# The order of a first stage, its loads and its band means, and a half group of matmuls at a later joint

## The chip, the cores and the metric

The kernel runs on one core of one Trainium2 chip. The metric is the device time of one execution in microseconds (us). Three runs of the kernel before gave 1173.47, 1173.22 and 1169.82 us: the median is 1173.22 us.

## The reference

Two layers of a diffusion backbone, for 512 latent tokens and 256 context tokens of 1024 channels. Layer 0 mixes tokens by centred means over windows of 2, 4, 8 and 16 tokens (one window for each group of 256 channels), layer 1 by attention. Cut to layer 0's first half:

```
sh1, sc1, gt1, sh2, sc2, gt2 = split(silu(cond) @ w_ada + b_ada, 6)     # one cond for latents, one for context
h = rms_norm(x, g_mix_pre) * (1 + sc1) + sh1
y = concat_g((window_mean_g(h_g) - h_g) @ w_pool[g]) * pool_scale        # four groups of 256 channels
x = x + gt1 * rms_norm(y, g_mix_post)
m = square(relu((rms_norm(x, g_mlp_pre) * (1 + sc2) + sh2) @ w_mlp_in)) @ w_mlp_out
x = x + gt2 * rms_norm(m, g_mlp_post)
```

Layer 1 has attention (`w_qkv`, `w_o`) in the place of the pooling, the same MLP, and for the output only the latents. All data are float32.

## The kernel before

**Numbers in two halves.** A product is made of float32r operands: each operand is split into a high part (a CAST on ACT) and a low part (a subtraction on DVE), and three matmuls (high·high, high·low, low·high) stand for one. "hi" and "lo" below are these two steps; `hH`/`hL` (in `ra`) hold an activation's halves, `rb` and `units` hold weights'.

**Tokens and stages.** Tokens lie in tiles of 128: tiles 0 to 3 are latents, 4 and 5 context. The first stage, which the diff rewrites, does this: (1) load x; normalise each tile; (2) multiply each tile by a band matrix, which gives "window mean minus the token" for every channel block k of 128 (PSUM tiles `psm` for latents and `psc` for context, opened for two blocks at a time); (3) load the conditioning weights `w_ada` in 20 loads of 1 MB and form shift, scale and gate: `ada_mm` (tile `psada`), `ada_rows` (a transpose on DVE), `ada_sel` (four tiny matmuls), then `mods`, `avec`, `minus` on DVE; (4) `centred`: scale and shift the means into `hH` (ACT) and `hL` (DVE); (5) the mixer `pool_a` (tile `pspool`): for each token tile and each group g six matmuls of 256 columns with the pooling weights; (6) its mean square, gate (`psg` are the gate's rows), residual, and the next norm; (7) `turn0`/`mod0`: transposes (`psx`), second modulation and split; (8) the first MLP group `psin`, begun in pieces of two channel blocks as they come ready.

**The joint.** At about 820 us attention's output projection (`psy`) ends and layer 1's MLP begins: token tiles 2 and 3 are normalised, turned and modulated (`norm_pair`) while the first MLP group `Inner(0, ...)` works on tiles 0 and 1 (`part(0, f)`), then on tiles 2 and 3 (`part(1, f)`). The group after it is multiplied in 512 columns at once.

**What sets the order.** Steps are put in a list with times (`st.at`), sorted and emitted in that order. A scheduler then moves instructions unless they are kept in program order; `Kept` keeps all of PE's instructions up to time 48 of the list and DVE's and ACT's up to 47.3 (`ordered`, `mixed`). Loads go through SP, in program order while `pinned`; a load waits until its buffer is free. Conditioning loads use a pool of four 1 MB buffers (`rawe`); the three buffers of `rawp` hold the pooling weights, two copies of the means (`stage`) and the MLP weights.

Of the kernel before, what the change touches and what calls it, by code (L numbers as in the profile page):

```python
# [37 lines left out]


# [29 lines left out]
def backbone(ctx: ExitStack, tc, x, ctx_in, w_ada, w_pool, pool_scale, w_qkv, g_q, g_k, w_o, w_mlp_in,  # L69
# [48 lines left out]

    def raw_load(src, pool=None):
        t = (pool or pools[0]).tile([P, 2048], F32, tag="raw", name="raw")  # L120
        d = sy.dma_start(t, src)
        if pinned[0]:
            tc.keep_in_program_order(d)
        return t
# [94 lines left out]
    def ada_mm(i, m, j, w=2):  # L219
        ps = psB.tile([P, 512], F32, tag="b", name="psada")  # L220
        kn = 2048 // (w * P)
        for z in range(KT // kn):
            raw = raw_load(w_ada[i, m, j + z]).rearrange("p (k n) -> p k n", n=w * P)
            for k in range(kn):
                at = kn * z + k
                q = 32 * (at % 4)
                te.matmul(ps[q:q + 32, 0:w * P], cond[:, at, :], raw[:, k, :], start=(at < 4), stop=(at >= 4))  # L227
        rowsd[i, m, j] = ps, w
# [12 lines left out]
    def ada_sel(i, m, j):  # L241
        ps, rows, w = rowsd.pop((i, m, j))
        out_ = ps[:, 0:2 * w]
        ada_turn(out_, rows.rearrange("p (b a x) -> p a x b", a=4, x=32)[:, :, 0:2, :], 2)
        ada_out(i, m, j, out_, 2, w)
# [52 lines left out]
    def gate_rows(i, m, ci, halves=(0, 1)):  # L298
        gc = gate_cols(i, m, ci, *((4 * halves[0], 4 * halves[-1] + 4)))
        for h in halves:  # L300
            ps = psB.tile([P, 512], F32, tag="b", name="psg")
            for k in range(4):
                te.matmul(ps[:, k * P:(k + 1) * P], gc[:, 4 * h + k:4 * h + k + 1].broadcast_to([P, P]), ident,
                          start=True, stop=True)
            sc.copy(gate[:, ci, 512 * h:512 * h + 512], ps)
# [16 lines left out]

    slot = [0] * NL + [1] * (NT - NL)
# [11 lines left out]
    def modulated_pair(t, i, s, hi, lo, works, wide, fine, on_act):  # L335
# [16 lines left out]
        for q in range(4):  # L352
# [13 lines left out]
            elif q % 2:  # L366
                ks = slice(2 * q - 2, 2 * q + 2)
                h = works[q // 2].rearrange("p (k n) -> p k n", n=256)
                sc.copy(place(hi, ks), h)
                ve.tensor_tensor(out=place(lo, ks), in0=h, in1=place(hi, ks), op=ALU.subtract)  # L370
# [11 lines left out]
    def mod0(t, q, on_act=(True, False)):  # L382
        ci, ps = 0 if t < NL else 1, turned.pop((t, q))
        for kk in range(2):
# [3 lines left out]
            if on_act[kk]:  # L388
# [5 lines left out]
        hi, lo = (z.rearrange("p k (h q n) -> p k q h n", h=2, n=P)[:, ks, t // 2] for z in (hH, hL))  # L394
        sc.copy(hi, h)
        ve.tensor_tensor(out=lo, in0=h, in1=hi, op=ALU.subtract)
# [25 lines left out]
    stage = {}  # L422

    def band_ev(k, q, on_act):
        if k not in stage:
            z = rawp.tile([P, 2048], F32, tag="raw", name="stage")
            stage[k] = z[:, 0:2 * TOK].rearrange("p (u n) -> p u n", n=TOK)
        t0, ln = SEGS[q]
        (sc.copy if on_act else ve.tensor_copy)(stage[k][:, :, t0:t0 + ln], (lat, con)[q][k])
        if q:  # L430
            for u in range(2):
                means[k + u] = [stage[k][:, u, t0:t0 + ln] for t0, ln in SEGS]

    rs, mix, yg, first = {}, {}, {}, []
# [7 lines left out]
    def centred(k, part):  # L442
        for ci, (t0, ln) in enumerate(SEGS):
            hi, lo, m = hH[:, k, t0:t0 + ln], hL[:, k, t0:t0 + ln], means[k][ci][:, 0:ln]
# [34 lines left out]
    def pool_a(t, gs=range(4), small_banks=False):  # L479
        if t not in mix:  # L480
            if small_banks:
                mix[t] = [psB.tile([P, 512], F32, tag="b", name="pspool") for _ in range(2)]
            else:
                pp_ = psA.tile([P, 2, 512], F32, tag="a", name="pspool")
                mix[t] = [pp_[:, 0, :], pp_[:, 1, :]]
        sl = slice(t * P, (t + 1) * P)
        for g in gs:
            seq = [(a, b, k) for k in (2 * g, 2 * g + 1) for a, b in ((hH, wp3H), (hH, wp3L), (hL, wp3H))]
            for n, (a, b, k) in enumerate(seq):
                te.matmul(mix[t][g // 2][:, (g % 2) * 256:(g % 2 + 1) * 256], a[:, k, sl], b[:, k, :],  # L490
                          start=(n == 0), stop=(n == len(seq) - 1))

    def pool_ms(t):
        pss = mix[t]
        ss = sm_tile("ss")
        for q in range(2):
            mean_square(pss[q], ss[:, q:q + 1])
        rs[t] = rstd(ss, 2)

    def pool_c(t):  # L500
        for q in range(2):
            sc.copy(accv[:, t, 512 * q:512 * q + 512], mix[t][q])
            mix[t][q] = accv[:, t, 512 * q:512 * q + 512]

    def pool_b(t, qs=range(2)):
        for q in qs:
            gated(t, accv[:, t, :], mix[t][q], 512 * q, 512 * q + 512)
# [22 lines left out]
    def norm_pair(t, i, s, hi, lo, wide, fine, on_act):  # L530
        modulated_pair(t, i, s, hi, lo, [accv[:, t, :], accv[:, t + 1, :]], wide, fine, on_act)
# [6 lines left out]
    def chunks1(g):  # L538
        if g == 0:
            return [[(0, 0, 0, 256)], [(1, 0, 256, 256)]], [(0, 2, 256, 0)]  # L540
# [4 lines left out]
    class Inner:  # L545
        def __init__(self, g, w, aH, aL, hid, chunks_of, ntok):
            self.w, self.a, self.ntok = w, (aH, aL), ntok
# [4 lines left out]
        def part(self, c, f, ks=range(KT)):  # L552
            (wH, wL), (aH, aL) = self.w, self.a
            if f not in self.ps:
                self.ps[f] = psA.tile([P, 2, 512], F32, tag="a", name="psin")
            ps, fs = self.ps[f], slice(f * P, (f + 1) * P)
            for k in ks:
                for n, (w, a) in enumerate(((wH, aH), (wH, aL), (wL, aH))):
                    for bank, o, t0, ln in self.chunks[c]:
                        start = k == 0 and n == 0  # L560
                        if ln is None:
                            ln, rhs = 256, a[:, k].rearrange("p (h q n) -> p q h n", h=2, n=P)[:, t0]
                            start = start and (f, bank) not in self.opened
                            self.opened.add((f, bank))
                        else:
                            rhs = a[:, k, t0:t0 + ln]
                        te.matmul(ps[:, bank, o:o + ln], w[:, k, fs], rhs, start=start,  # L567
                                  stop=(k == KT - 1 and n == 2), skip_group_check=len(ks) < KT)
# [157 lines left out]

    st = Steps()
    for t in range(NT):
        st.at(4.6 + 1.3 * t, rows_a, t)
    landing = ((19.3, 21.4, 22.4), (23.8, 25.9, 27), (27.1, 28.15, 28.7), (28.9, 30.0, 30.5), (31.4, 32.4, 33.4),  # L730
               (33.7, 34.8, 35.2), (40.6, 42.65, 43.9), (44.2, 46.25, 47.2),
               (47.75, 48.5, 49.5), (52.8, 53.2, 54.7), (60.5, 61.5, 62), (62.9, 63.9, 64.4), (65.2, 66.2, 66.7), (67.7, 68.7, 69.2))
    for zs, (m, j, w) in zip(landing, CONDITIONING):
        for z, fn, also in zip(zs, (ada_mm, ada_rows, ada_sel), ((w,), (), ())):
            st.at(z, fn, 0, m, j, *also)
    st.at(0, ordered.__setitem__, 0, True)
    st.at(0, mixed.__setitem__, 0, True)
    st.at(47.3, mixed.__setitem__, 0, False)
    st.at(48, ordered.__setitem__, 0, False)
    for t, z in enumerate((7.8, 9.7, 11.2, 12.7, 14.2, 16)):  # L740
        st.at(z, rows_b, t)
    for k in (0, 2):
        st.at(7.9, band_open, k)
    for t, z in enumerate((8.6, 9.9, 11.3, 13, 14.6, 18.2)):
        st.at(z, band_mm, t, range(4))
    for q, k, z in ((0, 0, 14.9), (0, 2, 14.9), (1, 0, 19.35), (1, 2, 19.35)):
        st.at(z, band_ev, k, q, k == 0)
    for k in (4, 6):
# [741 lines left out]
```

## Time and profile before

| | value |
|---|---|
| median of three runs | 1173.22 us |
| the profiled execution, own time | 1175.43 us |
| its span, first to last instruction | 1173.6 us |
| PE busy | 1147.6 us, 98% of the span |
| DVE busy | 934.4 us, 80% |
| ACT busy | 625.9 us, 53% |
| mean granted TensorE clock | 0.993 |

The profile is of one execution. Engines: PE is TensorE (PEld its weight loads), DVE VectorE, ACT ScalarE, POOL GpSimd, SP the queue that issues transfers. Times within it count from the span's start. In a line of the order of time the columns are start, duration, engine, source line, operation, output tile `<-` input tiles, shape, count, and in brackets the idle time ahead of it and what ended that. In the first stage most instructions carry the line of the helper `Kept` (L65 before), so tiles tell them apart. A float32 matmul with a full-precision operand (`psada`, `psc`, `psg`) shows as two records. In the table of stretches PEclk is the granted clock as a share of full speed.

### The profile page before, as it was taken

What the parts mean: (1) busy time and instruction counts of PE and PEld (TensorE: products, weight loads), DVE (VectorE), ACT (ScalarE), POOL (GpSimd) and SP (SyncE); (2) the same over time, 40 slices, a digit from 0 to 9 for tenths busy, and PEclk for the clock granted to TensorE, in tenths of its full rate; (3) what the DMA queues carried; (4) which work ended last, traced back from release to release, by engine and by line L of the source; (5) the groups of instructions that cost most, each with busy time, mean ns of one, the idle gap of its engine ahead of it and who ended that gap; (6) DMA issues with size and microseconds to landing.
All of it is one profiled execution on the core that took longest, in us unless ns stands there. A gap on an engine that the chain in (4) does not pass through costs nothing.

```text
span 1173.6 us, 15880 instructions
## 1 busy us (share of the span) xinstructions
PE 1147.6 (98%) x6124; PEld 993.3 (85%) x6124; DVE 934.4 (80%) x1518; ACT 625.9 (53%) x1067; POOL 68.6 (6%) x120
## 2 busy tenths in 40 slices
PE   7899999999999999999999999999899999999997
PEld 5679898899898988998888889998888888888886
DVE  4587687989988998897777599877687779778876
ACT  4576655454454435555585367753676436535522
POOL 2030000000000000000242200001100000000001
PEclk9899999999999999999999999999999999999999
DMA  9885114343444434343423100115134124304212
GB/s 368 329 321 181 50 59 144 117 155 129 144 144 144 144 116 147 115 144 126 180 72 108 37 1 37 37 73 214 73 135 153 59 85 144 108 36 144 108 36 108
DMA packets 25517, 147.32 MB, mean 126 GB/s; under 512 B 2785, under 2 KB 5217, under 8 KB 9698
## 3 DMA queue, kind: packets, MB, share of 16 engines
q1 hardware_dynamic: 25442, 146.32, 34.5%
q8 instruction: 48, 0.79, 0.3%
q14 instruction: 27, 0.22, 0.1%
HBM read 138.96 MB, written 7.34 MB: 125 GB/s over the span
## 4 chain that ended last, share of the span: by engine, by line
PE 49%; issue 42%; POOL 3%; DVE 3%; DMA 2%; ACT 1%; SPq 0%; POOLq 0%; DVEq 0%; ACTq 0%
PE pso L822 22%; PE psin L691 18%; PE psin L567 3%; PE psq L1067 2%; DMA raw<-in_w_ada 1%; PE pspool L65 1%; POOL rs L185 1%; PE psada L65 1%; PE pspool L490 1%; POOL rs L1076 1%; DMA xr<-in_x 1%; PE psada L227 1%; DVE ra L65 0%; POOL ms L183 0%; ACT junk L170 0%
## 5 line engine op out<-in xcount | busy, mean ns | idle before, releaser
L822 PE MATMUL pso<-units,rb 128*128 128x512 f32 x1152 | 278.2, 392 | 0.0
L822 PEld LDWEIGHTS pso<-units,rb 128*128 128x128 f32 x1152 | 214.8, 188 | 41.2
L273 DVE SCALAR_TENSOR_TENSOR rows<-raw,cond,rows 128x256 f32<-128x256 f32 x280 | 126.8, 476 | 2.0
L834 DVE TENSOR_TENSOR acc<-acc,pso 128x512 f32<-128x512 f32 x129 | 85.2, 675 | 41.2 <-PE pso L822 41.0
L567 PE MATMUL psin<-ra,rb 128*128 128x512 f32 (+1 forms) x432 | 104.7, 343 | 1.8 <-ACT ra L364 1.6
L926 PE MATMUL pso<-units,pairs 128*128 128x512 f32 x336 | 82.3, 389 | 0.0
L567 PEld LDWEIGHTS psin<-ra,rb 128*128 128x128 f32 x432 | 71.2, 193 | 11.3 <-ACT ra L364 1.9
L567 PE MATMUL psin<-ra 128*128 128x512 f32 x256 | 80.4, 389 | 0.0
L926 PEld LDWEIGHTS pso<-units,pairs 128*128 128x128 f32 x336 | 63.1, 188 | 13.1
L930 DVE TENSOR_TENSOR acc<-acc,pso 128x512 f32<-128x512 f32 x72 | 48.7, 681 | 28.8 <-PE pso L926 28.8
L183 POOL TENSOR_SCALAR ms<-ss 128x1 f32<-128x1 f32 x20 | 10.7, 533 | 998.0 <-ACT junk L170 943.9
L691 PE MATMUL psin<-ra,units 128*128 128x384 f32 x336 | 65.6, 337 | 0.4 <-ACT psin L703 0.4
L691 PE MATMUL psin<-sums,units 128*128 128x384 f32 x336 | 63.9, 337 | 0.0
L691 PEld LDWEIGHTS psin<-ra,units 128*128 128x128 f32 x336 | 59.7, 188 | 3.9 <-ACT psin L703 0.9
L691 PEld LDWEIGHTS psin<-sums,units 128*128 128x128 f32 x336 | 58.9, 188 | 1.7
L143 DVE TENSOR_TENSOR units<-raw,units 128x1024 fp32r<-128x1024 f32 (+2 forms) x49 | 55.1, 1149 | 3.9 <-ACT units L140 3.7
L567 PEld LDWEIGHTS psin<-ra 128*128 128x128 f32 x256 | 48.1, 188 | 9.9
L140 ACT CAST units<-raw 128x1024 fp32r<-128x1024 f32 (+2 forms) x49 | 46.8, 995 | 14.3 <-PE pso L822 10.2
L567 PE MATMUL psin<-rb 128*128 128x512 f32 (+1 forms) x144 | 53.4, 372 | 0.2 <-DVE rb L365 0.2
L832 ACT COPY acc<-pso 128x512 f32<-128x512 f32 x48 | 27.1, 587 | 49.0 <-PE pso L822 48.6
L1067 PE MATMUL psq<-units,ra 128*128 128x512 f32 x216 | 51.6, 392 | 0.0
L567 PE MATMUL psin<-rb,ra 128*128 128x512 f32 x128 | 49.8, 389 | 0.0
(280 smaller groups left out, 2344.6 us busy)
## 6 DMA issues: line engine op xcount, KB each, us to landing
raw<-in_w_ada SPq DMA_DIRECT2D x48, 1024.0 KB, 5.1
raw<-in_w_mlp_in SPq DMA_DIRECT2D x32, 1024.0 KB, 4.9
raw<-in_w_mlp_out SPq DMA_DIRECT2D x32, 1024.0 KB, 5.8
raw<-in_w_qkv SPq DMA_DIRECT2D x6, 1024.0 KB, 4.8
spill<-xr SPq DMA_DIRECT2D x10, 512.0 KB, 4.9
xr<-spill SPq DMA_DIRECT2D x10, 512.0 KB, 6.6
raw<-in_w_o SPq DMA_DIRECT2D x4, 1024.0 KB, 4.9
xr<-in_x SPq DMA_DIRECT2D x4, 512.0 KB, 6.2
```

The source lines that it names most:

```text
L65: return lambda *args, **kw: self.tc.keep_in_program_order(f(*args, **kw))
L140: a = sc.copy(hi, raw)
L143: b = ve.tensor_tensor(out=lo, in0=raw, in1=hi, op=ALU.subtract)
L273: ve.scalar_tensor_tensor(out=r, in0=raw[:, k, :], scalar=cond[:, k, c:c + 1], in1=r, op0=ALU.mult, op1=ALU.add)
L567: te.matmul(ps[:, bank, o:o + ln], w[:, k, fs], rhs, start=start, stop=(k == KT - 1 and n == 2), skip_group_check=len(ks) < KT)
L691: te.matmul(bank, w[k], a[k], start=start and k == 0 and m == 0, stop=stop and k == 3 and m == 2, skip_group_check=True)
L822: te.matmul(pss[h][:, 0:cols[h][1]], a[:, f, ts_], w[:, f, cols[h][0]:sum(cols[h])], start=(n == 0 and not seeded[t]), stop=(n == len(seq) ...
L832: sc.copy(d, ps)
L834: ve.tensor_tensor(out=d, in0=d, in1=ps[:, 0:w], op=ALU.add)
L926: te.matmul(ps, a, w, start=(m == 0), stop=(m == len(seq) - 1))
L930: ve.tensor_tensor(out=M[n][:, t], in0=M[n][:, t], in1=ps, op=ALU.add)
L1067: te.matmul(ps, a[:, k, sl], w[:, k % 4, :], start=(k == 0 and n == 0), stop=(k == KT - 1 and n == 2))
```

## The change

**First stage.** The conditioning loads take seven buffers: a list `turns` says for each of the 20 loads whether it goes to `rawe` (0) or to `rawp` (1), and the 1 MB of the first MLP weights is loaded behind the twelfth conditioning load, where it stood behind the eighteenth. The means no longer use `rawp`: `band_ev` copies those of all eight blocks (before: of blocks 0 to 3) from PSUM into `acc`, whose normalised rows have been read by then. The mixer works on tiles 5, 4 and 0 together as groups of `hH`/`hL` become ready, then on 1, 3 and 2. From list time 24.5 on, everything up to the end of the first MLP group is emitted in the order of one table, `FIRST`, and kept in it on PE, DVE and ACT (`ordered` and `mixed` end at 100). A halved load (`mm:SH1_0a`) and each of gate, split, evacuation and modulation is a word of its own in it.

**Joint.** The second MLP group of layer 1 has half of its weights split earlier (`half_early`), and its product for tiles 0 and 1 (24 matmuls of 256 columns) is put into the joint; a `paired` group keeps both halves f in one PSUM tile, in 256-column pieces. The split of the upper half of tiles 0 and 1 (`upper_half`) is emitted later, and the first group's product is cut in two for it. In `squares` both activations of the first two groups come after all of a group's matmuls.

```diff
+FIRST = """
+psc45 ev6 mm:SH1_0a ev4c psc67 mm:SH1_0b ev6c rows:SH1_0 mm:SC1_2 sel:SH1_0 rows:SC1_2 mods:SH1_0 sel:SC1_2 hi:0
...
     def raw_load(src, pool=None):
+        if pool is None and turns:
+            pool = (pools[0], rawp)[turns.pop(0)]
...
     def band_ev(k, q, on_act):
-        if k not in stage:
-            z = rawp.tile([P, 2048], F32, tag="raw", name="stage")
...
+        to = accv[:, (0, NL)[q]:(NL, NT)[q], P * k:P * k + 256]
+        (sc.copy if on_act else ve.tensor_copy)(to, (lat, con)[q][k].rearrange("p u (a n) -> p (u a) n", n=256))
...
-    def pool_a(t, gs=range(4), small_banks=False):
+    def pool_a(t, g):
         if t not in mix:
-            if small_banks:
+            if t in (4, 1):
                 mix[t] = [psB.tile([P, 512], F32, tag="b", name="pspool") for _ in range(2)]
...
     def chunks1(g):
-        if g == 0:
-            return [[(0, 0, 0, 256)], [(1, 0, 256, 256)]], [(0, 2, 256, 0)]
+        if g < 2:
+            return [[(0, 0, 0, 256)], [(0, 256, 256, 256)]], [(0, 1, 512, 0)]
...
+            if self.paired and not self.ps:
+                t = psA.tile([P, 2, 512], F32, tag="a", name="psin")
+                self.ps = {q: t[:, q:q + 1, :] for q in range(2)}
...
+    turns.extend((0, 0, 0, 0, 1, 1, 0, 0, 1, 0, 0, 1, 0, 0, 1, 0, 0, 1, 0, 0))
...
-    for z, t, g in ((30.6, 4, 0), (32.5, 4, 1), (35.4, 4, 2), (36.2, 5, 0), (36.3, 5, 1), (36.4, 5, 2), (42.6, 4, 3), (42.62, 5, 3)):
-        st.at(z, pool_a, t, (g,), t == 4)
...
+    for n, what in enumerate(FIRST.split()):
+        st.at(24.5 + n / 1000, step, what)
+    st.at(100, ordered.__setitem__, 0, False)
+    st.at(100, mixed.__setitem__, 0, False)
...
         def squares(inner, q):
+            for f in range(2) if inner.paired else ():
+                for c in range(2):
+                    if (c, f) not in begun[inner]:
+                        inner.part(c, f)
             for f in range(2):
-                inner.part(len(inner.chunks) - 1, f)
+                if not inner.paired:
+                    inner.part(0, f)
                 sc.activation(F[:, q, f, :], inner.relu(f), AF.Square)
...
-        wi = [None, w_in(1, 1, ins[1], True)]
+        put((hi[:, :, P:], lo[:, :, P:]), raw1[0][:, :, P:], True)
...
+    def half_early():
+        hi, lo = (rb[:, z:z + 1024].rearrange("p (k n) -> p k n", n=P) for z in (4096, 5120))
+        sc.copy(hi, raw1[0][:, :, 0:P])
...
+        at(41.65, upper_half)
         for f in range(2):
-            at((41, 42)[f], lambda *a: first1[0].part(*a), 0, f)
+            for h in range(2):
+                at(41.7 + f / 10 + h, lambda *a: first1[0].part(*a), 0, f, range(4 * h, 4 * h + 4))
...
+        for h in range(2):
+            at((47.5, 47.6)[h], lambda ks: first1[1].part(0, 0, ks), range(4 * h, 4 * h + 4))
```

PE before, from the first mixer matmuls of the first stage on (`psada<-raw,cond` is a load's product, `psada<-rows,sel` and `psada<-work,sel` are `ada_sel`, `pspool` is the mixer):

```order
L65 MATMUL pspool<-rb,ra 128x256 x6
L65 MATMUL psada<-raw,cond 32x256 x8
L65 MATMUL pspool<-rb,ra 128x256 x6
L65 MATMUL psada<-rows,sel 32x2x2 x4
L65 MATMUL psada<-raw,cond 32x256 x8
L65 MATMUL psada<-rows,sel 32x2x2 x4
L65 MATMUL pspool<-rb,ra 128x256 x24
L65 MATMUL psada<-raw,cond 32x512 x8
L65 MATMUL pspool<-rb,ra 128x256 x12
```

PE in the same place with the change:

```order
L87 MATMUL psada<-raw,cond 32x256 x16
L87 MATMUL psada<-rows,sel 32x2x2 x4
L87 MATMUL pspool<-rb,ra 128x256 x12
L87 MATMUL psada<-rows,sel 32x2x2 x4
L87 MATMUL psada<-raw,cond 32x256 x8
L87 MATMUL pspool<-rb,ra 128x256 x6
L87 MATMUL psada<-rows,sel 32x2x2 x4
L87 MATMUL psada<-raw,cond 32x512 x4
L87 MATMUL pspool<-rb,ra 128x256 x18
L87 MATMUL psada<-raw,cond 32x512 x4
L87 MATMUL pspool<-rb,ra 128x256 x12
```

The first mixer matmuls moved behind two more load products, and 36 mixer matmuls (tiles 5, 4 and 0) now stand ahead of the first gate load's second half, where 12 stood ahead of the whole load.

PE at the joint before, around the transposes of tiles 2 and 3 (`psin_7408` and `psin_7442` are the two halves f of the first group, `psx` the transposes):

```order
L567 MATMUL psin_7442<-rb_100 128x256
L567 MATMUL psin_7442<-ra_99,rb_100 128x256
L350 MATMUL psx_7475<-ident_87,acc_86 128x128 x3
L350 MATMUL psx_7480<-ident_87,acc_86 128x128 x3
L350 MATMUL psx_7485<-ident_87,acc_86 128x128 x3
L350 MATMUL psx_7490<-ident_87,acc_86 128x128 x3
L567 MATMUL psin_7408<-ra_99,rb_100 128x256
```

With the change (`psin_7420` is the first group, `psin_7513` the second):

```order
L608 MATMUL psin_7420<-ra_99,rb_100 128x256
L608 MATMUL psin_7513<-rb_100 128x256
L608 MATMUL psin_7513<-ra_99,rb_100 128x256 x2
L385 MATMUL psx_7477<-ident_87,acc_86 128x128 x3
L385 MATMUL psx_7482<-ident_87,acc_86 128x128 x3
L385 MATMUL psx_7487<-ident_87,acc_86 128x128 x3
L385 MATMUL psx_7492<-ident_87,acc_86 128x128 x3
L608 MATMUL psin_7513<-rb_100 128x256
L608 MATMUL psin_7513<-ra_99,rb_100 128x256
L608 MATMUL psin_7420<-ra_99,rb_100 128x256
```

Of the second group's 24 matmuls 22 stand ahead of the twelve transposes; before, nothing but the first group's 48 stood there.

ACT right behind the joint's modulation before (L140 and L898 split weights, L578 is the first group's ReLU out of PSUM):

```order
L140 CAST ra<-raw 128x2048
L898 CAST ra<-raw 128x1024
L578 ACTIVATE work<-psin 128x512
L917 ACTIVATE hid<-work 128x512
L578 ACTIVATE work<-psin 128x512
L898 CAST ra<-work 128x1024
L898 CAST units<-raw 128x1024
```

With the change (L166 splits the weights of the third group, L619 is the ReLU):

```order
L954 CAST ra<-raw 128x8x128
L954 CAST ra<-raw 128x1024
L954 CAST ra<-work 128x1024
L954 CAST units<-raw 128x1024
L166 CAST rb<-raw 128x2048
L619 ACTIVATE work<-psin 128x512 x2
L978 ACTIVATE hid<-work 128x512 x2
```

Both ReLUs of the first group moved behind the split of the third group's weights, which waits for a load.

276 lines of the change are left out of this document (160 added, 116 removed).

## The prediction

> **What bounds the kernel now.** The page first, for the engine that decides:
>
> ```profile
> PE 1147.6 (98%) x6124; PEld 993.3 (85%) x6124; DVE 934.4 (80%) x1518; ACT 625.9 (53%) x1067; POOL 68.6 (6%) x120
> ```
>
> PE works in 98% of the span, so the kernel can only gain where PE stands still or runs slowly. The waits of PE between 24 and 106 us, where the rewritten order lies, come second:
>
> ```profile
> PE psada L65 <- DMA raw<-in_w_ada: 1.9, 1, 1.9
> PE psada L65 <- DVE rows L65: 1.4, 2, 0.9
> PE pspool L65 <- DVE mods L65: 0.8, 1, 0.8
> PE pspool L65 <- DVE ra L65: 0.8, 1, 0.8
> PE psada L227 <- DVE mods L249: 0.7, 1, 0.7
> PE psg L65 <- DVE gc L292: 0.6, 1, 0.6
> ```
>
> These longest ones add up to 6.2 us; none is longer than 1.9. Third, busy time and granted clock by stretches (length, then busy time and count of PE, PEld, DVE, ACT, POOL; then PEclk, DMA share, GB/s):
>
> ```profile
> 24.40:28.00 3.60, 1.66 (x17) 0.32 (x16) 2.14 (x2) 0.68 (x1) 0.00 (x0) 1.00 1.01 419
> 28.00:31.40 3.40, 3.40 (x28) 2.17 (x24) 0.85 (x2) 0.00 (x0) 0.00 (x0) 0.50 1.01 422
> 31.40:38.20 6.80, 5.94 (x83) 3.82 (x75) 5.17 (x16) 6.47 (x11) 0.00 (x0) 1.00 1.01 402
> 38.20:41.60 3.40, 1.89 (x28) 0.82 (x26) 2.68 (x7) 0.67 (x2) 0.00 (x0) 1.00 1.03 373
> 41.60:48.40 6.80, 5.81 (x36) 5.53 (x40) 3.56 (x9) 2.93 (x6) 0.00 (x0) 0.50 0.61 233
> 48.40:105.00 56.60, 55.20 (x524) 44.23 (x524) 41.27 (x73) 37.49 (x73) 11.81 (x24) 1.00 0.73 279
> 834.00:836.90 2.90, 1.30 (x12) 1.10 (x11) 0.75 (x1) 0.51 (x2) 0.79 (x2) 1.00 0.33 134
> 836.90:840.30 3.40, 1.54 (x11) 1.10 (x10) 3.24 (x7) 3.40 (x8) 0.00 (x0) 1.00 0.00 0
> 840.30:843.80 3.50, 3.50 (x19) 3.50 (x18) 2.64 (x4) 2.98 (x3) 0.00 (x0) 0.51 0.02 5
> ```
>
> A stretch loses its length minus PE's busy time, and at clock 0.50 half of its busy time too. First stage: 1.9 + 1.7 + 0.9 + 1.5 + (1.0 + 2.9) + 1.4 = 11.3 us. Joint: 1.6 + 1.9 + 1.7 = 5.2 us. These are the bounds of what each part of the change can win.
>
> **First stage, until the loads let go.** Half clock and idle time up to 48 us have one root, the loads. The queue runs at 402 to 422 GB/s up to 38 us. Four loads, each with its issue and, below, the us from issue to landing (the second half of the first shift at 10.79, the load ahead of it, and two behind):
>
> ```profile
> 9.51 0.33 SPq L121 DMA_DIRECT2D raw<-in_w_ada  x1
> raw<-in_w_ada SPq DMA_DIRECT2D x1, 1024.0 KB, 14.0
> 10.79 0.33 SPq L121 DMA_DIRECT2D raw<-in_w_ada  x1
> raw<-in_w_ada SPq DMA_DIRECT2D x1, 1024.0 KB, 16.6
> 21.20 0.33 SPq L121 DMA_DIRECT2D raw<-in_w_ada  x1
> raw<-in_w_ada SPq DMA_DIRECT2D x1, 1024.0 KB, 8.7
> 25.53 0.33 SPq L121 DMA_DIRECT2D raw<-in_w_ada  x1
> raw<-in_w_ada SPq DMA_DIRECT2D x1, 1024.0 KB, 9.3
> ```
>
> They land at 23.5, 27.4, 29.9 and 34.8, with one more between the last two, so one per 2.45 us behind 27.4, on a queue that is full already. More buffers do not move these. So the start of centring stays too: with the change PE takes the 29.9 load's product (1.07, second row below) before the shift's `ada_sel`, and centring starts near 31.8, against 31.73 before:
>
> ```profile
> 31.73 4.90 ACT L65 ACTIVATE ra<-stage,phase,avec 128x512 fp32r<-128x512 f32 x8 [6.65 <-DVE phase L65]
> 32.94 1.07 PE L65 MATMUL psada<-raw,cond 128*32 128x256 f32 x16
> ```
>
> What changes is where PE's small pieces lie. The context bands now fill the 1.9 us ahead of the 27.4 landing. In exchange PE has little but loads' products behind it, some 1.1 us each: done with the first near 28.6 it waits 1.3 us for 29.9, done with the second and an `ada_sel` near 31.1 it waits 1.2 for 32.35, done with the third near 33.4 it waits 1.4 for 34.8. I keep 3.9 us of waiting. From 35.9 on mixer work is ready: `hH` of blocks 0 and 1 is done at 31.8 + 2 x 1.22 (4.90 for four blocks), and DVE follows within another 1.22 or so, at about 35.4. Before, PE did 12 mixer matmuls up to 42.9 and waited for the last blocks; now it has 36 and a gate load's half to do in that time.
>
> The copies of the means of blocks 4 to 7 out of PSUM are new on ACT, four operations. By the nearest row, 4.90 for eight operations of similar size, they are 2.4 us (bounds 0.6 each and twice that, as one copies 1024 columns). ACT is idle for 6.65 us ahead of 31.73, in the same bracket; that hides them, at 0. Without that cover they would delay centring by the 2.4.
>
> **The clock.** PE's clock fell to half after stretches with PE busy 46% (1.66 of 3.60), 56% (1.89 of 3.40) and 45% (1.54 of 3.40); it came back after one full stretch, but not after the first half of 41.6 to 48.4. With the change PE is busy about 1.9 of the 3.4 us from 28 and about 1.0 of the next: I expect it halved during 34.8 to 38.2. There 0.8 us of waiting is over and some 2.6 us of mixer and load work run at half speed: 1.3 us. The Trainium skill, page "TensorE: Matmul & The Clock Gate", section "Part 1: The HAM clock gate (the "warmup" mystery)", puts the drop behind at least one idle window of about 3.4 us; by that rule nothing is halved here and the sum is 1.3 us lower. The trace disagrees: it halved three times, with no single wait over 1.9 us.
>
> **First stage, the rest.** From 38 us PE's queue holds work throughout; the mixer's rate is that of this group (48 to 105 us):
>
> ```profile
> L490 PE MATMUL pspool<-rb,ra 128*128 128x256 f32 x72 | 9.8, 288 | 0.0
> ```
>
> Six mixer matmuls are 0.8 us (9.8 for 72). Loads: the twelfth lands at 48.5 before (41.25 + 7.3, last rows of this part) because its buffer was late; with seven buffers at 47.2, and the last, nine further on, near 47.2 + 9 x 2.45 = 69.3. PE wants that one near 81, so 11 us cover the transfer of the first MLP weights, which now has eight loads behind it instead of two.
>
> ```profile
> 41.25 0.33 SPq L121 DMA_DIRECT2D raw<-in_w_ada  x1
> raw<-in_w_ada SPq DMA_DIRECT2D x1, 1024.0 KB, 7.3
> ```
>
> New on all three engines is that nothing may pass what waits. Followed along the table with these durations, four places are tight: the first transposes of tiles 0/1 wait for a norm on DVE; those of the third quarter wait for a PSUM bank that a modulation frees; the first `psin` waits until tile 3's gate frees its bank (all later MLP pieces queue behind it on PE); the last shift load's product waits for a modulation on ACT. Each is 0 to 0.6 us. I set 1.8 us, the old 1.4 and a little (bounds 0 and 5.0: on top of the 1.4, four waits of 0.9, the longest on DVE above). Left of the 11.3 are 3.9 + 1.3 + 1.8 = 7.0; the stage gains 4.3 us, and what follows, bound by PE as the page shows, moves up with it.
>
> **The joint.** PE waits twice, for the norm of tile 3 and for the modulation of its transposes; the first line also times the twelve transposes:
>
> ```profile
> 835.87 1.53 PE L350 MATMUL psx<-ident,acc 128*128 128x128 f32 x12 [1.60 <-DVE acc L528]
> 839.03 0.50 PE L567 MATMUL psin<-ra,rb 128*128 128x256 f32 x2 [1.64 <-ACT ra L364]
> 828.03 0.30 PE L567 MATMUL psin<-rb 128*128 128x256 f32 x1
> 830.56 0.28 PE L567 MATMUL psin<-rb 128*128 128x256 f32 x1
> 847.08 0.40 PE L567 MATMUL psin<-rb,ra 128*128 128x512 f32 x1
> 857.30 0.39 PE L567 MATMUL psin<-rb,ra 128*128 128x512 f32 x1
> ```
>
> The two pairs of equal rows have 21 and 45 matmuls from start to start: 0.12 us for 256 columns, 0.227 for 512. The 24 matmuls put in are 2.9 us of later work, and the idle time is 3.5. But 22 of them (2.65 us) stand ahead of the transposes, whose input is ready 1.60 us after PE's old work: the transposes start about 1 us late. Behind them only two are left against the modulation's 1.64, so 1.3 us of waiting stays. The moved `upper_half` puts its low part behind tile 3's residual on DVE; PE reaches it about then: between 0 and a wait like the two above, 1.6; I take 0.3, since 37 matmuls, more than before, stand ahead of it. No stretch is half idle, so the clock stays up, which gives 1.7. The first two groups in 256-column pieces cost 48 x (2 x 0.12 - 0.227) = 0.6. The transposes' late start is in part paid back: without the moved split in its way, the norm of tile 3 is ready sooner, by up to that split's length (about 1 us); I count 0.2 of the late start. Of the 5.2 stay 0.2 + 1.3 + 0.3 + 0.6 = 2.4: a gain of 2.8.
>
> Behind it ACT's order has a trap: both ReLUs now wait behind the third group's weight split, whose load was issued at 844.69 (loads of its kind take 4.9 us to land, the median in the page). The first product started at 857.75 and its operand's last low part began at 854.70:
>
> ```profile
> 844.69 0.33 SPq L121 DMA_DIRECT2D raw<-in_w_mlp_in  x1
> raw<-in_w_mlp_in SPq DMA_DIRECT2D x32, 1024.0 KB, 4.9
> 854.70 0.68 DVE L898 TENSOR_TENSOR pairs<-work,pairs 128x512 fp32r<-128x512 f32 x1
> 857.75 5.60 PE L926 MATMUL pso<-ra,pairs 128*128 128x512 f32 x24
> ```
>
> Slack was 2.4 us. Now PE arrives about 3 us earlier; the load is issued near 844.0 (its buffer frees after half a split, not a whole one) and lands at 848.9. Behind it ACT and DVE have a split, two ReLUs, two squares and the operand's halves, some 5.7 us of single operations of up to 2 us each: about 854.6, where PE comes at 854.7. I put the cost at 0; with a load of 8 us it is 3.
>
> **Sum.** 4.3 + 2.8 = 7.1 us. Against the profiled execution, 1173.6 us of span and 1175.43 us of own time, that is 1166.5 and 1168.3; that execution is 2.2 us above the median of the runs. Against the median: 1173.2 - 7.1, about 1166 us. A measurement of this kernel can tell about 0.3% (3.5 us) from no change: faster means below 1169.7.
>
> **The rivals.**
> - *The clock stays full in the first stage.* As the skill's rule would have it, but by this kernel's own rows too (834 to 836.9 was 45% busy and not followed by half clock): 1.3 us more, and fewer tight waits: 1163 to 1165.
> - *The fill does not fill.* The scheduler put 22 of 24 matmuls ahead of the transposes; if ReLU or operand come late by 3 us as well, the joint wins nothing: 1173.2 - 4.3 = 1169. For it: ACT's order above. Against: 5 us loads in that quiet stretch.
> - *The first stage gives its gain back.* With up to eight loads in flight the early ones land later: between the loads issued at 9.5 and 10.79 the landings lay 3.9 us apart (23.5 and 27.4), not 2.45, just after two more had been issued. Another 3 us of that and 1.4 of order waits leave the joint alone: 1170.4.
> - *Slower.* The clock, at both places: if 55% busy halves it and PE's many short waits on the other engines keep it halved, from 31 to about 57 us, then 21 us of work from 36 on take 10.5 us more than at full clock, instead of the 1.3 I set: -4.3 + 9.2 = +4.9; at the joint two such stretches cost 3.4, where I won 2.8, 0.6 worse than none: 1173.2 + 5.5, about 1179. It decides if PE is under some 70% busy beyond 38 us. Against it: after 38 us the queue always holds ready mixer work, and before, 55.20 of 56.60 us were busy.
>
> **How the numbers follow.** Forecast 0.42, full clock 0.20, no joint 0.12, joint alone 0.14, slower 0.10, the order not doing what it says 0.02 (no change). The predicted time is the forecast's, 1166. The range: fast end, only the loads' 3.9 stay (7.4) and 4.2 at the joint, 1161.5; slow end, the joint alone and a little less, 1171.5; it leaves out the slower case and the tails. Faster: 0.42 + 0.20 + 0.12 and a fifth of 0.14, about 0.77; the rest of 0.14 and 0.02 are within 0.3%, 0.13; slower 0.10.
>
> **What would show it.** Right: PE waits three times for `in_w_ada` between 28 and 35, the second group's first matmul starts near 100.8 instead of 105.1, the joint shows one wait of about 1.3 us and clock 1.00. Wrong: half clock beyond 38.2, a DMA wait on PE after 45, a wait of `pso` for `pairs` right after the joint, or waits of PE above 3 us in all between 48 and 101.

## The result, and the profile after

The changed kernel takes 1165.83 us (median of 7 runs, 1164.73 to 1166.60), the kernel before 1169.82 us in the 7 runs beside it (1169.20 to 1173.47; the three from which the base was set are among them). The ratio is 0.9951, 95% interval 0.9936 to 0.9965: 5.7 us by the ratio, 4.0 us by the medians. The forecast was 1166 us and a gain of 7.1 us.

The profiled execution of the changed kernel took 1164.73 us, that of the kernel before 1175.43: 10.7 us apart, far more than the medians. Three instructions on PE divide both executions: the first matmul of layer 0's second MLP group (end of the first stage), the first of the joint, and the last product. First the kernel before, then the changed one, in order of time:

```profile
105.08 16.81 PE L567 MATMUL psin<-ra,units 128*128 128x384 f32 x96
827.91 0.28 PE L567 MATMUL psin<-ra,rb 128*128 128x256 f32 x1
1165.88 0.88 PE L822 MATMUL pso<-units 128*128 128x256 f32 x6
```

```profile
97.25 16.91 PE L608 MATMUL psin<-ra,units 128*128 128x384 f32 x96 [0.25 <-ACT work L615]
820.05 0.28 PE L608 MATMUL psin<-ra,rb 128*128 128x256 f32 x1
1155.20 0.88 PE L878 MATMUL pso<-units 128*128 128x256 f32 x6
```

The first stage is 7.8 us shorter (105.08 to 97.25), the stretch from there to the joint is alike (722.83 and 722.80), and from the joint to the end it is 2.8 us less (337.97 and 335.15). The changed kernel by the stretches of the prediction (length, busy time and count of PE, PEld, DVE, ACT, POOL; PEclk, DMA share, GB/s), with its own joint as the last row:

```profile
24.40:28.00 3.60, 3.60 (x31) 1.88 (x29) 1.81 (x2) 2.32 (x4) 0.00 (x0) 1.00 1.02 419
28.00:31.40 3.40, 1.67 (x40) 1.03 (x37) 1.71 (x6) 0.59 (x1) 0.00 (x0) 1.00 1.01 422
31.40:38.20 6.80, 5.39 (x81) 3.84 (x82) 5.95 (x16) 6.62 (x12) 0.00 (x0) 1.00 1.02 420
38.20:41.60 3.40, 3.25 (x34) 2.22 (x33) 3.37 (x9) 2.29 (x5) 0.00 (x0) 1.00 1.01 412
41.60:48.40 6.80, 6.80 (x60) 4.70 (x60) 2.23 (x6) 2.94 (x7) 0.22 (x1) 1.00 1.01 422
48.40:105.00 56.60, 55.39 (x509) 47.07 (x508) 44.67 (x71) 44.27 (x74) 13.44 (x23) 1.00 0.72 283
828.00:832.10 4.10, 2.70 (x25) 2.50 (x23) 2.01 (x5) 2.61 (x6) 0.00 (x0) 1.00 0.01 4
```

The idle time has moved from 24 to 28 us to 28 to 35 us, where PE waits for loads, and the clock is 1.00 in every row. Next come PE's two longest sums of waits from 24 to 106 us. Behind them, for the joint, are the transposes of tile 3, the one wait of size that follows them, and on DVE the norm (L562) that the transposes need:

```profile
PE psada L87 <- DMA raw<-in_w_ada: 2.6, 3, 1.4
PE psada L87 <- DVE mods L87: 1.5, 3, 0.7
```

```profile
828.97 1.47 PE L385 MATMUL psx<-ident,acc 128*128 128x128 f32 x12
832.07 0.51 PE L608 MATMUL psin<-ra,rb 128*128 128x256 f32 x2 [1.40 <-ACT ra L399]
826.08 0.75 DVE L562 TENSOR_SCALAR acc<-xr,rs 128x1024 f32<-128x1024 f32 x1 [1.10 <-POOL rs L211]
```

### The profile page after: what moved, and what is told of

Same layout as the page of the kernel before. It is cut to its first block, busy times and chain, and to the rows that moved or that the text cites. A ratio compares the mean times of both kernels' runs of the same rounds, so it can differ in the third digit from the quotient of the medians.

```text
span 1163.0 us, 15973 instructions
## 1 busy us (share of the span) xinstructions
PE 1140.5 (98%) x6172; PEld 990.2 (85%) x6172; DVE 934.0 (80%) x1515; ACT 630.0 (54%) x1068; POOL 69.7 (6%) x120
## 4 chain that ended last, share of the span: by engine, by line
PE 63%; issue 29%; DVE 3%; DMA 2%; ACT 2%; POOL 1%; SPq 0%; POOLq 0%; DVEq 0%; ACTq 0%
PE pso L878 22%; PE psin L732 18%; PE psq L1133 5%; PE psy L1393 3%; PE po L1368 3%; PE pss L1327 2%; PE pspt L1349 2%; PE pspool L87 2%; PE psin L87 1%; PE psin L608 1%; PE psada L87 1%; DMA raw<-in_w_ada 1%; POOL rs L211 1%; DMA xr<-in_x 1%; ACT junk L196 0%
## 5 line engine op out<-in xcount | busy, mean ns | idle before, releaser
L608 PE MATMUL psin<-ra,rb 128*128 128x512 f32 (+1 forms) x320 | 90.1, 358 | 1.4 <-ACT ra L399 1.4
L608 PE MATMUL psin<-ra 128*128 128x512 f32 (+1 forms) x256 | 76.5, 376 | 0.0
L608 PEld LDWEIGHTS psin<-ra,rb 128*128 128x128 f32 x320 | 57.2, 189 | 10.3 <-ACT ra L399 1.6
L608 PE MATMUL psin<-rb 128*128 128x512 f32 (+1 forms) x160 | 57.2, 359 | 0.2 <-DVE rb L400 0.2
L166 ACT CAST units<-raw 128x1024 fp32r<-128x1024 f32 (+2 forms) x49 | 46.9, 996 | 17.9 <-PE pso L878 13.7
L608 PE MATMUL psin<-rb,ra 128*128 128x512 f32 (+1 forms) x128 | 48.1, 376 | 0.0
```

Of the source, the lines that this page charges most:

```text
L166: a = sc.copy(hi, raw)
```

## The experiments

The question was why two single executions differ by 10.7 us and the medians by 4.0. Each kernel's ratio is to the kernel before in the same series of runs, where that one's median was 1170.5 to 1170.6 us.

**The kernel before again** (no edit).

> The kernel before, unchanged, for a second profile. Theory A (the sum of the prediction): half clock belongs to the order of the work, so a second profile shows it at the same three places (behind 24.6 to 28.0, behind 38.2 to 41.6, behind 836.9 to 840.3), span about 1173.6 us. Theory B (phase): the clock is judged in stretches of 3.41 us that start at another point in each execution (0.66 us past a multiple in the profile of before, 2.20 in that of after), and a thin place halves the clock only where a whole stretch falls into it; then the second profile shows half clock at other places, fewer of them, and a span shorter by up to 1.7 us for each 3.41 us of half clock that is gone: 1168 to 1172.

Measured: 1170.67 us (12 runs, 1169.25 to 1175.81), ratio 1.0010 (0.9996 to 1.0024), no difference, as it should be. Its profile has one halved stretch of 3.41 us ahead of the end where the first had four: the second group starts at 101.97, and the joint takes 336.52 us to the last product. With 27 more runs of the kernel before from the same series there are 39. Each run has a mean granted clock:

| mean clock | runs | time, us | median |
|---|---|---|---|
| 0.999 | 17 | 1169.25 to 1170.55 | 1169.51 |
| 0.998 | 6 | 1170.52 to 1171.02 | 1170.58 |
| 0.997, 0.996 | 8 | 1170.78 to 1173.30 | |
| 0.995 | 5 | 1173.12 to 1174.48 | 1173.57 |
| 0.993 | 3 | 1175.01 to 1175.81 | 1175.06 |

A fitted line gives 0.95 us for each 0.001. The profile from which I predicted (0.993) belongs to the rarest row. The mean also holds half clock at the very end of the program, 1.9 to 5.0 us of it in the 14 profiles. So 0.999 leaves no room for a halved stretch ahead of the end, but 0.998 can come from the end alone, as in the profile with four buffers below. The half clock comes in pieces of 3.41 us on a grid: in the first profile at 27.97, 41.62 and 840.34, the second four and the third 238 steps of 3.413 behind the first; in this one the grid lies elsewhere. Here are the stretch on this grid ahead of the halved one, the halved one, and the joint's two, which were not followed by half clock:

```profile
37.60:41.01 3.41, 1.69 (x32) 0.94 (x28) 3.02 (x9) 0.18 (x1) 0.00 (x0) 1.00 0.99 406
41.01:44.42 3.41, 3.41 (x19) 3.41 (x18) 1.65 (x3) 2.76 (x6) 0.00 (x0) 0.50 0.91 375
829.49:832.90 3.41, 1.81 (x16) 1.61 (x15) 0.92 (x2) 1.15 (x2) 0.79 (x2) 1.00 0.38 154
832.90:836.31 3.41, 1.77 (x14) 1.39 (x13) 2.42 (x5) 3.02 (x7) 0.00 (x0) 1.00 0.00 0
```

In the first profile the joint's two stretches on its own grid were these, and the second was followed by half clock at 840.34:

```profile
833.51:836.92 3.41, 1.82 (x17) 1.62 (x16) 0.75 (x1) 1.03 (x3) 0.79 (x2) 1.00 0.38 154
836.92:840.34 3.41, 1.55 (x12) 1.11 (x11) 3.28 (x7) 3.41 (x8) 0.00 (x0) 1.00 0.00 0
```

The joint's waits are the same two of 1.6 us as before, but cut by the grid into 53% and 52% busy instead of 53% and 45%. This fits theory B, and not theory A: the same waits cost a halved stretch or not, by where the grid falls. The Trainium skill, page "TensorE: Matmul & The Clock Gate", section "Part 1: The HAM clock gate (the "warmup" mystery)", says that the window of 3413 ns runs freely and does not start with the kernel; the traces agree (0.66, 0.05 and 2.20 us past a multiple of 3.413 in three of them).

**The first stage alone, and the joint alone.** The first has the changed kernel with the joint's edits taken back, the second the kernel before with only those.

```diff
 # first stage alone, against the changed kernel
-        wi = [None, None]
+        wi = [None, w_in(1, 1, ins[1], True)]
...
-        at(41.65, upper_half)
...
-        at(36, half_early)
...
 # joint alone, against the kernel before: the same lines the other way round
```

> The change of the first stage alone; the joint is the one before. Theory A: the first stage wins 4.3 us, 1169.8 - 4.3 = 1165.5. Theory B: without half clock the kernel before loses only waits, 6.7 us between 24.4 and 105, and the changed one 4.5: it wins 2.2 us, about 1167.6. In the profile of either: PE's idle time from 24 to 105 about 4.5 us, the joint's two waits of 1.6 us back.

> The change of the joint alone; the first stage is the one before. Theory A: it wins 2.8 us, 1169.8 - 2.8 = 1167.0. Theory B: waits at the joint go from 3.5 to 1.6 us and 0.6 us of smaller pieces is added, so it wins 1.3 us, about 1168.5; only where half clock falls behind the joint of the kernel before it wins 1.7 more. In the profile: no wait for the norm of tile 3, one wait of about 1.4 us for the modulation.

Measured: first stage alone 1167.65 us, ratio 0.9967 (0.9956 to 0.9977); joint alone 1169.95, ratio 0.9991 (0.9981 to 1.0001), not told from no change. Theory B's numbers were 1167.6 and 1168.5, theory A's 1165.5 and 1167.0. In the profile of the joint alone the joint is 335.17 us long, 1.35 less than in the second profile of before. Its runs won less than theory B has it. Eleven of the 12 had a clock of 0.997 or less, against 10 of the 27 of the kernel before beside them. That half clock took the rest of the gain is argued from these clocks, not shown; why it came so often, with the first stage of before unchanged, stays open. The first stage alone shows the half clock that I had forecast for 34.8 to 38.2, in this execution:

```profile
31.12:34.54 3.42, 1.70 (x36) 0.81 (x32) 2.62 (x10) 2.39 (x4) 0.00 (x0) 1.00 1.01 419
34.54:37.95 3.41, 3.19 (x30) 2.39 (x31) 3.22 (x8) 2.99 (x6) 0.00 (x0) 0.50 1.01 420
```

At clock 0.999 its runs are 1166.06 to 1166.78 (median 1166.41 of 4), against 1169.51 for the kernel before: 3.1 us that owe nothing to a halved stretch.

**Four buffers.**

```diff
-    turns.extend((0, 0, 0, 0, 1, 1, 0, 0, 1, 0, 0, 1, 0, 0, 1, 0, 0, 1, 0, 0))
+    turns.extend([0] * 20)
```

> The changed kernel with all conditioning loads in the four old buffers, everything else as changed, so the written order stays. If the order carries the gain of the first stage: within 1 us of the changed kernel, 1165 to 1167. If the three added buffers carry it: loads behind the first eight wait for their buffers, PE waits for them between 40 and 65 us, 3 to 6 us in all, and the time is 1168.5 to 1172.

Measured: 1166.78 us, ratio 0.9963 (0.9949 to 0.9977), and in its profile:

```profile
PE psada L87 <- DMA raw<-in_w_ada: 1.7, 2, 1.4
97.65 14.66 PE L608 MATMUL psin<-ra,units 128*128 128x384 f32 x83 [0.24 <-ACT work L615]
```

The second group starts 0.4 us later than with seven buffers, and PE waits for loads no more than there. The written order carries the first stage's gain; three more buffers are worth 0.4 us in the profile, and in the medians at most about 1.

**Throwaway matmuls in the kernel before, twice.** The first adds 7 and 4 repeats of load products and 3 small matmuls, the second 7, 3 and 1. What the repeats write is written over, and the small ones go to columns that nobody reads. The second's edit:

```diff
+            for k in {(0, SH1, 0, 0): (0, 1, 2, 3, 0, 1, 2), (0, SC1, 3, 0): (0, 0, 0)}.get((i, m, j, z), ()):
+                te.matmul(ps[32 * k:32 * k + 32, 0:w * P], cond[:, k, :], raw[:, k, :], start=True, stop=True)
...
+    st.at(33.45, warm, 1)
```

> The kernel before with throwaway matmuls in PE's waits of the first stage (7 and 4 load products twice over, 3 small ones into spare columns; their results are written over or never read), so that no stretch of 3.41 us there is under some 70% busy. Theory B (an aligned stretch at about half busy halves the clock): no half clock between 24 and 48 us, the mean clock 0.998 to 0.999 in nearly every run, median 1169.3 to 1169.9 where the kernel before had 1170.6, and no run above 1172. Rival (something else there halves it, the full transfer queue for one): the spread of the kernel before stays, 1169.3 to 1175.8, and the added work costs up to 0.5.

> The kernel before with 11 throwaway matmuls (7 repeats of a load product in the wait before 27.4 us, 3 repeats of another and one small one between 38 and 41.6); PE's order is otherwise the same row for row, which it was not in the first such kernel. Theory B (an aligned stretch of 3.41 us at about half busy halves the clock): the two places of the first stage are at 70% or more and no longer halve it, mean clock 0.998 to 0.999 in nearly every run (the joint is left as it is), median 1169.3 to 1169.9, no run above 1172.5, where the kernel before spreads from 1169.3 to 1175.8 with a median of 1170.6. Rival (another cause of half clock there): spread and median as before.

Measured: 1175.09 us, ratio 1.0038 (1.0023 to 1.0052), and 1174.68, ratio 1.0024 (1.0010 to 1.0038). Neither came out as theory B had it. In the first, PE's order behind 60 us changed too, and PE waits 1.7 us there for a modulation. The second keeps the order, but its repeats took longer than planned: the group of 16 rows that the prediction shows with 1.07 us became

```profile
34.23 2.35 PE L65 MATMUL psada<-raw,cond 128*32 128x256 f32 x22
37.21:40.63 3.42, 2.16 (x28) 0.95 (x26) 2.32 (x7) 0.00 (x0) 0.00 (x0) 1.00 0.99 398
40.63:44.04 3.41, 2.08 (x16) 2.03 (x17) 1.70 (x5) 1.64 (x3) 0.00 (x0) 0.50 0.95 344
```

1.28 us for three repeats instead of 0.4, so all behind it came later (its only run at 0.999 took 1171.16). In this profile the wait at 24 to 28 us did not halve the clock, but the stretch at 37.21, 63% busy, did. So a busy share over a half is no protection, and the prevention that theory B promised was not shown (the last section has a nearer measure of busy).

**Throwaway matmuls in the changed kernel.**

```diff
-... ev6c rows:SH1_0 mm:SC1_2 sel:SH1_0 rows:SC1_2 mods:SH1_0 sel:SC1_2 hi:0
-mods:SC1_2 mm:SH1_2 hi:1 ...
+... ev6c rows:SH1_0 warm:4 mm:SC1_2 sel:SH1_0 warm:3 rows:SC1_2 mods:SH1_0 sel:SC1_2 warm:4 hi:0
+mods:SC1_2 mm:SH1_2 warm:9 hi:1 ...
```

> The changed kernel with 20 throwaway mixer-size matmuls (0.136 us each, 2.7 us) in PE's waits between 28.3 and 33.9 us. Theory B: no half clock left in the first stage, median 1164.7 to 1165.2 where the changed kernel had 1165.8, spread under 1.2 us. Rival (the clock is not what spreads the changed kernel's runs): no gain, 1165.8, or up to 0.5 slower where the added work delays a product.

Measured: 1165.23 us (1164.44 to 1166.42), ratio 0.9956 (0.9943 to 0.9968). In its profile PE is busy without a break from 24 to 48 us and the second group starts at 96.96, yet the runs spread by 2.0 us, where the changed kernel had 1.9 and theory B under 1.2: not told from the changed kernel.

**The joint without its fill.**

```diff
-        wi = [None, None]
+        wi = [None, w_in(1, 1, ins[1], True)]
...
-        at(36, half_early)
-        for h in range(2):
-            at((47.5, 47.6)[h], lambda ks: first1[1].part(0, 0, ks), range(4 * h, 4 * h + 4))
```

> The changed kernel without the second group's half at the joint (its weights are split where the kernel before split them, in 512-column matmuls); the moved split of the upper half and the pieces of the first group stay. If the fill carries the joint's gain: PE waits about 1.6 us for the norm of tile 3 and 1.6 us for the modulation as before, less 0.3 us for 24 larger pieces, and the time is 1.0 to 1.5 above the changed kernel's, about 1167. If the moved split carries it: the wait for the norm is under 0.8 us, and the time within 0.5 of 1165.8.

Measured: 1167.64 us, ratio 0.9971 (0.9961 to 0.9981). That is the time of the case in which the fill carries the gain, but the waits are others:

```profile
827.59 0.38 PE L608 MATMUL psin<-rb 128*128 128x256 f32 x1 [1.36 <-DVE rb L1457]
830.44 1.47 PE L385 MATMUL psx<-ident,acc 128*128 128x128 f32 x12
833.55 0.38 PE L608 MATMUL psin<-ra,rb 128*128 128x256 f32 x1 [1.64 <-ACT ra L399]
```

L1457 is the moved split's low part. The move of the split traded the norm's 1.60 us for 1.36 us one step earlier, and in the changed kernel the fill covers that.

**Two other places for the fill.** First 6 ahead of the transposes and 18 behind them; then 15 ahead of the first group's second half, the transposes in its middle, 12 of it and 9 put-in ones behind them. Both pin the transposes of tile 3 and matmuls around them (`tc.keep_in_program_order`).

```diff
 # 6 and 18
-            at((47.5, 47.6)[h], lambda ks: first1[1].part(0, 0, ks), range(4 * h, 4 * h + 4))
+            at((47.3, 47.6)[h], lambda ks: first1[1].part(0, 0, ks), (range(2), range(2, 8))[h])
 # 15, and 12 + 9
...
+            at((42.7, 47.5)[f], lambda *a: first1[0].part(*a), 0, f, range(4, 8), True)
...
+            at((42.6, 47.6)[h], lambda ks: first1[1].part(0, 0, ks, True), (range(5), range(5, 8))[h])
```

> The changed kernel with only 6 of the 24 put-in matmuls ahead of tile 3's twelve transposes and 18 behind them, kept in that order (in the changed kernel it is 22 and 2). If the transposes start late in the changed kernel because of the fill, as the prediction has it: they start 1.5 to 2 us earlier, the 18 cover the modulation, the wait of 1.40 us goes, and the time is 1.2 to 1.6 below the changed kernel's, about 1164.4. If the norm is not ready earlier: the wait moves ahead of the transposes (1 us or more) and nothing is won, 1165.8.

> The changed kernel with the put-in matmuls of the joint in another order: 15 ahead of the second half of the first group (where the moved split's low part is waited for), tile 3's transposes in the middle of that half, 12 of the first group and 9 put-in ones behind the transposes. If the two waits (low part 1.4, modulation 1.6) each need their own 1.4 us of cover: no wait at the joint over 0.3 us, the joint 1.4 to 1.7 us shorter, about 1164.2. If the norm of tile 3 then comes late: a wait of about 1 us ahead of the transposes, and 0.5 won.

Measured: 1165.07 us, ratio 0.9954 (0.9941 to 0.9967) for the first. The modulation's wait is gone, and the low part's is back, which neither case of the expectation had; the joint is 334.83 us long, 0.3 less than in the changed kernel:

```profile
826.78 0.39 PE L610 MATMUL psin<-rb 128*128 128x256 f32 x1 [1.38 <-DVE rb L1465]
830.36 1.47 PE L385 MATMUL psx<-ident,acc 128*128 128x128 f32 x12
```

The second order covers both: 1163.56 us (1162.70 to 1163.78), ratio 0.9926 (0.9908 to 0.9945). No wait of PE is left in its list between 810 and 870 us. The norm ends at 826.63, and PE arrives at 826.69:

```profile
825.88 0.75 DVE L564 TENSOR_SCALAR acc<-xr,rs 128x1024 f32<-128x1024 f32 x1 [1.11 <-POOL rs L211]
826.69 1.53 PE L385 MATMUL psx<-ident,acc 128*128 128x128 f32 x12
```

From the joint to the last product it takes 333.33 us, 1.8 less than the changed kernel. Its slowest run (1163.78) is faster than the fastest of the changed kernel in the same series (1165.79, next experiment): this order beats both.

**The changed kernel again, and both fills together** (no edit; the edits of the last order and of the throwaway matmuls).

> The changed kernel, unchanged, for a second profile and more runs. Theory B: its first stage has one thin stretch left (28 to 34 us), so some executions show one stretch of half clock at 32 to 38 us; median 1165.4 to 1166, spread under 2.5 us.

> The order of the joint as in the kernel just above, and the 20 throwaway matmuls in the waits of the first stage from the earlier run. Theory B: no half clock left in either place; about 1163.6 median with a spread under 1 us, faster than the changed kernel by 1.5 to 2.2 us. If the throwaway work wins nothing: equal to the kernel above, 1164.2.

Measured: 1166.51 us (1165.79 to 1167.32), ratio 0.9953 (0.9935 to 0.9972), half a microsecond above what theory B gave, and 1164.12 (1163.58 to 1164.40), ratio 0.9931 (0.9911 to 0.9951). The throwaway work wins nothing on top of the order. The second profile of the changed kernel has its half clock at the joint, not in the first stage:

```profile
831.23:834.65 3.42, 1.80 (x13) 1.39 (x13) 3.42 (x7) 3.42 (x8) 0.00 (x0) 1.00 0.00 0
834.65:838.06 3.41, 3.41 (x19) 3.41 (x18) 3.40 (x5) 1.61 (x2) 0.00 (x0) 0.50 0.20 29
```

The wait of 1.4 us, with one of 0.2 behind it, is enough where the grid falls badly. With it the joint takes 336.67 us to the last product instead of 335.15. The reordered joint runs spread by 1.1 us, the changed kernel's by 1.5 in the same series.

## Why the prediction was right, and where it was not

The time, the sign and the range held; that the time came out within 0.2 us was in part luck. Two terms were mis-sized in opposite directions.

- **The clock was the term that failed.** I counted half clock as part of the kernel: 4.6 us of the first stage's 11.3 and 1.7 of the joint's 5.2 were its cost, and of the 7.1 us gain 5.0 came from it (4.6 - 1.3 + 1.7). Over 39 runs the kernel before has a median of 1170.57 against 1169.51 at a mean clock of 0.999: half clock costs its typical run 1.1 us, not 6.3. The changed kernel still meets it: in three of the seven profiles with the new first stage and no throwaway work a stretch starting between 34.4 and 35.5 us is halved, as I had forecast, and in the second profile of the changed kernel one at the joint. Its 13 runs have a mean clock of 0.9975, the 39 before 0.9973, so no typical gain from the clock is shown. In these runs the slow tail is gone: the slowest took 1175.8 us before and takes 1167.3 now.
- **The waits were worth more than I had counted.** Without the clock my sum is 1.0 us for the first stage and 1.1 for the joint. Measured: 3.1 (runs at 0.999) and 1.4 (336.52 to 335.15 in the profiles; the runs of the joint alone show 0.6, not told from nothing). Of the first stage's, 1.6 us is waiting between 24 us and the second group: 6.1 idle in the second profile of before and 4.5 in the first of the changed kernel. Here are first the one, then the other.

```profile
24.00:48.00 24.00, 19.30 (x198) 12.29 (x197) 15.20 (x34) 10.84 (x19) 0.00 (x0) 0.93 0.89 359
48.00:101.97 53.97, 52.56 (x503) 43.06 (x502) 40.64 (x72) 37.59 (x73) 11.85 (x24) 1.00 0.75 291
```

```profile
24.00:48.00 24.00, 20.71 (x234) 13.66 (x233) 15.46 (x37) 14.77 (x26) 0.00 (x0) 1.00 1.01 419
48.00:97.25 49.25, 48.04 (x469) 39.72 (x467) 39.38 (x65) 38.42 (x67) 13.66 (x24) 1.00 0.74 292
```

 For the other part my sum had no term: PE's busy time in these rows falls from 71.9 us, 70.2 without the halved stretch's 1.7, to 68.8. The changed kernel has the same matmuls in longer runs of one kind. Two kinds, up to the second MLP group's start, in the second profile of before and then the changed kernel, at full clock in both:

```profile
L567 PE MATMUL psin<-ra,rb 128*128 128x256 f32 x144 | 19.2, 288 | 0.1
L379 PE MATMUL psx<-ident,acc 128*128 128x128 f32 x48 | 7.2, 279 | 0.0
```

```profile
L87 PE MATMUL psin<-ra,rb 128*128 128x256 f32 x144 | 18.5, 286 | 0.0
L87 PE MATMUL psx<-ident,acc 128*128 128x128 f32 x48 | 6.4, 277 | 0.0
```

 The 1.5 us between these pairs is too much for the two: where kinds alternate, their records overlap, and a kind's row counts the overlap that the other kind's row counts too. With each moment given only to the matmul that started last, I get about 0.7 us from the trace. That the gathering does it is argued from the order, not tried alone.
- *Until the loads let go.* Right in kind: PE waits three times for `in_w_ada` between 28 and 34 us. They add up to 2.6 us, not 3.9, and centring starts at 30.80 instead of 31.8. But part of this was the profile from which I predicted: the four loads that landed there at 27.4 to 34.8 us landed at 26.4, 28.9, 31.4 and 33.9 in the second profile of before, where centring starts at 29.37. With the change they land at 26.2, 28.7, 31.2 and 33.7, so that more buffers do not move the early loads held. The start of centring did not stay, as I had said; against that second profile it is 1.4 us later. The four copies of the means cost nothing, as set: ACT still idles for 2.89 us ahead of centring. The four-buffer run shows that the buffers matter little later as well.
- *The tight places* behind 48 us: 1.2 us idle against the 1.8 set.
- *The second group's start*: 97.25, where I said 100.8. Half clock was absent in that execution; at full clock the kernel before would have started near 100.3 (101.97 less one halved stretch of 1.7).
- *The joint.* One wait of 1.40 us and, in the first profile, a clock of 1.00, as forecast (1.64 less two matmuls of 0.12 is 1.40; my sum had 1.3). In the second profile the clock fell there nonetheless, so the 1.7 us that I counted for it are not safe. The transposes start 2.1 us after the norm's end (826.83 to 828.97) rather than 1; for the moved split's low part I had 0.3 and it is 0, but only because the scheduler put 13 of the 22 in front of it: without them it is 1.36 to 1.38.
- *ACT's order behind it* costs nothing, as set: both ReLUs ran behind the third group's split, and the operand's last low part still ends 1.85 us (847.03 to 848.88) ahead of its product.

```profile
840.83 1.90 ACT L166 CAST rb<-raw 128x2048 fp32r<-128x2048 f32 x1 [0.74 <-DMA raw<-in_w_mlp_in]
842.64 1.08 ACT L619 ACTIVATE work<-psin 128x512 f32<-128x512 f32 x2
846.34 0.69 DVE L954 TENSOR_TENSOR pairs<-work,pairs 128x512 fp32r<-128x512 f32 x1
848.88 1.07 PE L987 MATMUL pso<-ra,pairs 128*128 128x512 f32 x4
```

- *The rivals.* In the profiled execution the clock did stay full (1164.73 us, the rival's 1163 to 1165). The slower case needed half clock far beyond 38 us; in no profile with the new first stage does a halved stretch of it start behind 36 us. The early loads did not land later with more of them in flight (26.2 to 33.7 us above), so the first stage did not give its gain back; and the fill does fill, as the run without it shows.
- *The base.* I set the gain against 1173.2, the median of three runs, two of them as long as the runs at 0.995 and 0.996 in the table. The larger base and the larger gain cancelled. That is the luck: against the median of 1169.8 the same 7.1 us would have given 1162.7, 3.1 below what was measured.

## What to carry to other kernels

Before a term for half clock goes into a sum, ask how often it happens: compare the profiled execution's mean clock and time with the other runs, and if it is one of the slow ones, weigh the term by how often it occurs. When a split or a norm is moved, look for the wait that it creates at its new place, and divide the fill by waits, each with its own length of cover; here the same 24 matmuls won 1.8 us more in a written order than where the scheduler had put them. Whether gathering small matmuls and transposes into runs pays by itself is worth a try of its own; here it was not separated from the order.

## What was not expected of the hardware

- A stretch of about half busy can halve the clock for the next 3.41 us, on a grid that lies differently in each execution. In 14 profiles, counting stretches that lay on the grid and had full clock themselves (16 to 110, 610 to 700, 820 to 850 us), all eight under 46% busy were followed by half clock, none above 63%; between 49% and 63% seven were and 29 were not. Busy time as the profile gives it does not tell those apart. A shorter one nearly does: a 256-column matmul is shown with 0.28 us, though the next starts 0.12 us behind it; if 0.16 us is taken off the end of every matmul, the fifteen stretches ahead of a drop are 29% to 43% busy, and of all others from 16 to 1150 us only two lie under 44% (39% and 40%, at 29.51 in the changed kernel and 27.89 in the reordered joint's profile). This is an estimate fitted to these traces, not a rule; by it the stretch at 37.21 in the kernel before with repeats was 42% busy. The Trainium skill, page "TensorE: Matmul & The Clock Gate", section "Part 1: The HAM clock gate (the "warmup" mystery)", puts the drop behind at least one idle window; the traces disagree, since none of the fifteen stretches ahead of a drop was idle (38% to 63% busy).
- Load products that go to four different quarters of 32 columns take 0.13 us each (1.07 for eight): in the trace four of them start within 0.02 us. Three in a row into the same quarter take 0.43 us each (1.28 for three).
